# Feed-forwards of a two-layer trunk: the norm's sums pinned in TensorE's order, weight chunks split eight ahead, two plain columns fewer

## The chip, the cores and the metric

The kernel runs on one core of a Trainium2 chip. The metric is the device time of one launch in microseconds (us), the median of several runs; before the change it is 2092.37 us (three runs, 2092.34 to 2093.55). Lower is better.

The engines of the core are TensorE (PE in the profile, its weight loads PEld), VectorE (DVE), ScalarE (ACT), GpSimd (POOL) and SyncE (SP). SP issues the loads of weights; POOL issues the DMAs that add to what lies in memory already ("accumulating" below). Each engine works through its own instructions in the order in which they stand.

## The reference

512 tokens of width 1024 go through two layers. In each layer four parts are added to x, each behind an RMS norm: a feed-forward with weight 1/2, a token mixer, a cross-attention into 256 memory tokens, and a second feed-forward with weight 1/2. What the change touches is the four feed-forwards:

```
def rmsnorm(x, g):
    return x * rsqrt(mean(x * x, -1) + EPS) * g
def swiglu(h, w1, w3, w2):
    return (silu(h @ w1) * (h @ w3)) @ w2
...
x = x + 0.5 * swiglu(rmsnorm(x, ffn1_norm[l]), ffn1_w1[l], ffn1_w3[l], ffn1_w2[l])
```

w1 and w3 are 1024 x 2816 (22 columns j of 128), w2 is 2816 x 1024. Everything is in float32.

## The kernel before, in words

**Layout.** x is kept transposed: eight tiles of 128 channels by 512 tokens (`xall` in the profile). A float32 product is made of three matmuls on rounded halves (`mm3`, L84 to L86): high by high, high by low, low by high. So each weight chunk (128x1024) is split on arrival into `whi` (ScalarE, L76) and `wlo` (DVE, L77), and each operand likewise.

**A norm ahead of its row.** A feed-forward starts before its 1/rms is known. `Norm.part` writes h = gain * x, split into high (ScalarE, L79) and low (DVE, L80), and the first columns are multiplied with this h. In the meantime `Norm.square` sums the squares of the eight channel tiles: the first goes to a tile of its own, `far` (ScalarE, L401), the next three are added to it by accumulating DMAs of POOL (L403), each of which waits for the one before; the fifth starts `sq`, the sixth is added to it and then `far` (DVE, L407 and L409), and the last two are added. The tiles of single squares come from a ring of four buffers. `Norm.tick` is called after every second k of a column product. At its tick `late` it issues the sum over the channels on TensorE (four small matmuls against ones, L346), from which DVE, POOL (power -1/2, `rcol`, L350) and DVE make diagonals `dg` (L357 to L362). `rest` ticks later two matmuls (L369) spread 1/rms over all partitions, ScalarE copies it out (`rrow`, L421), and the epilogues that waited for it (`left`, `right`, L688 to L700) run.

**Two kinds of columns.** The first `PLAIN` columns j of a feed-forward are plain: `col_matmul` makes the product with w1 and the one with w3, 24 matmuls of 128x512 each, and the epilogues multiply by the row. All others are taken two j at a time in the 2x2 Strassen-Winograd form (`Pairs.block`): seven half-size products in place of eight, for w1 and for w3 one block each, of 48 matmuls 128x256 and 12 pairs of matmuls of 512 and 256 columns (L554, L555). The blocks need operands that are made of x times the row (`operands`, DVE and ScalarE, in 14 steps between the plain columns), and sums of weights, one of them by an accumulating DMA of POOL (L134). `PLAIN` is 8, 6, 6, 6 for the four feed-forwards. The columns are made in `PARTS` of 8, 8 and 6; after each part its down-projection (`project`, L451) adds to x, in two halves of four channel tiles. In the last part's projection of a feed-forward the h and the squares of the next norm are made on the way (`late`, `after`): those of the first half's four tiles during the second half.

**Weights.** The list of all chunks is written down in advance (`Weights.src`). `next` hands one out, splits up to `SPLIT` = 5 chunks ahead of it (4 or 6 near blocks) and loads 7 ahead. Raw chunks, split chunks, h, `far`, blocks' operands and others share 38 slots of one pool, so that a load or a split waits until a slot is free.

**What sets the order.** A scheduler puts the instructions of each engine in an order by what is ready when, in its own reckoning, and by the order in which the code issues them. `tc.issue_after(x)` makes instructions of TensorE stand behind instruction x, without a semaphore. Before the change the feed-forwards' sums are not held to a place: two columns can be mixed, and L346 sinks behind them.

Of the kernel before, what the change touches and what calls it, by code (L numbers as in the profile page):

```python
# [14 lines left out]
P = 128  # L15
D = 1024
# [15 lines left out]
PLAIN = (8, 6, 6, 6)  # L32
# [14 lines left out]
def trunk_kernel(ctx: ExitStack, tc: tile.TileContext, ap: dict, out: bass.AP):  # L47
# [33 lines left out]

    def mm3(o, a, b, start, stop, more=False):

        pe.matmul(o, a[0], b[0], start=start, stop=False, skip_group_check=more)  # L84
        pe.matmul(o, a[0], b[1], start=False, stop=False, skip_group_check=more)  # L85
        pe.matmul(o, a[1], b[0], start=False, stop=stop, skip_group_check=more)  # L86


    class Weights:
# [3 lines left out]
        SPLIT, LOAD = 5, 7  # L93

        def __init__(self):
            self.src, self.raw, self.hl, self.at, self.todo = [], {}, {}, 0, []

# [17 lines left out]
        def ahead(self, i, n):  # L115

            m = 0
            while i < len(self.src) and m < n:
                yield i
                m += 2 if len(self.src[i]) == 2 else 1  # L120
                i += 1

# [81 lines left out]
        def next(self):  # L204
            i = self.at
            self.at += 1
            while self.todo:
                self.step()
            block = len(self.src[i]) == 2
            near = any(len(x) == 2 for x in self.src[i:i + 4])  # L210
            end = i >= len(self.src) - 9
            ahead = [*self.ahead(i, (6 if end else 4) if near else self.SPLIT)]
            for j in ahead:
                if j not in self.hl:
                    self.todo.append(self.cut(j))
                    if not block or j == i:
                        while self.todo:
                            self.step()
            for j in self.ahead(i, 5 if end else self.LOAD):
                self.load(j)  # L220
            return self.hl.pop(i)
# [10 lines left out]
    for l in range(L):  # L232
        for w1, w3, w2 in (("ffn1_w1", "ffn1_w3", "ffn1_w2"), ("ffn2_w1", "ffn2_w3", "ffn2_w2")):
            for lo, hi in PARTS:
# [89 lines left out]
    def prepare_mem():  # L324
# [13 lines left out]
        pr = col_to_row(dg, 2)  # L338
# [3 lines left out]
    def col_rsqrt(sq, inv, tag, tile=acc_tile):  # L342

        ps = tile()
        for i in range(NT):
            pe.matmul(ps[:, i:i + 1], sq[:, i * P:(i + 1) * P], ones[:, 0:1], start=True, stop=True)  # L346
# [4 lines left out]
        return col  # L351
# [13 lines left out]
    def col_to_row(dg, n=NT, tile=acc_tile):  # L365

        pr = tile()
        for c in range(2):
            pe.matmul(pr[:, :n * P], ones_r, dg[:, c, :n].rearrange("p a b -> p (a b)"), start=c == 0, stop=c == 1)  # L369
        return pr  # L370

    class Norm:
# [4 lines left out]
        def __init__(self, gain, l, row=True, late=2, rest=2, far=4):  # L377
            self.gain, self.l, self.row, self.late, self.rest, self.FAR = gain, l, row, late, rest, far
# [33 lines left out]
        def tick(self):  # L412
            self.ticks += 1
            if self.ticks == self.late:
                self.col = col_rsqrt(self.sq, 1.0 / D, "rcol")
                if self.row:
                    self.dg = diagonals(self.col)
            if self.ticks == self.late + self.rest and self.row:
                pr = col_to_row(self.dg)
                self.r = tp.tile([P, T], F32, tag="rrow", name="rrow", bufs=1)  # L420
                act.copy(self.r, pr)  # L421
                for fn in self.waiting:
                    fn()

# [38 lines left out]
    def col_matmul(ps, parts, n=T, tick=None):  # L463
        whl = wts.next()
        for k in range(NK):
            mm3(ps[:, :n], (whl[0][:, k, :], whl[1][:, k, :]), parts[k], start=k == 0, stop=k == NK - 1)
            if tick and k % 2:
                tick()
# [731 lines left out]
    norm = Norm("ffn1_norm", 0, late=1, rest=0, far=0)  # L1200
# [30 lines left out]
    for l in range(L):  # L1231
# [11 lines left out]
        norm, nxt = nxt, Norm("ffn2_norm", l)  # L1243
        xattn(l, norm, mn, nxt.add)
        norm = nxt
        if l + 1 < L:
            nxt = Norm("ffn1_norm", l + 1)
# [53 lines left out]
```

## Time and profile before

| | before |
|---|---|
| median of the runs | 2092.37 us |
| the profiled execution's own time | 2092.47 us |
| its span | 2090.7 us |
| TensorE busy | 2077.4 us, 99% |
| weight loads | 1798.0 us, 86% |
| DVE busy | 1408.4 us, 67% |
| ScalarE busy | 918.0 us, 44% |
| POOL busy | 230.3 us, 11% |
| mean granted clock of TensorE | 0.999 |

The span is cut from the first to the last instruction, the time of the run holds 1.8 us around it. A timeline row has the start in us, the duration, engine, line and operation, output<-inputs, sizes and a count; in brackets stands how long the engine was idle before, and what released it. Matmuls overlap: their pace is read from start to start, not from their duration. A row of windows has busy time and number of instructions for PE, PEld, DVE, ACT and POOL in turn, then the granted clock, the share of the DMA engines and GB/s.

### The profile page before, as it was taken

Reading aid. Unit: us, or ns where it says so; the run is one execution under the profiler, and the core shown is the slowest. Engines: PE = TensorE matmul, PEld = TensorE weight load, DVE = VectorE, ACT = ScalarE, POOL = GpSimd, SP = SyncE. Lnnn points to the kernel's source line nnn. Section 1 sums busy time; section 2 is a strip of 40 time slices with the busy share of each in tenths; the row PEclk is TensorE's granted clock in tenths of the full one; section 3 lists DMA queues with packets and bytes.
Section 4 is the critical chain, followed back from the end, with each engine's and each line's share of the span. In section 5 each row is a group of like instructions: output and inputs, shape, how many; then the busy total and the mean of one; then the engine's idle time right before and its main releaser. Section 6 shows DMA issues by size and latency. Waiting matters only on the chain.

```text
span 2090.7 us, 29622 instructions
## 1 busy us (share of the span) xinstructions
PE 2077.4 (99%) x11538; PEld 1798.0 (86%) x11538; DVE 1408.4 (67%) x2126; ACT 918.0 (44%) x1461; POOL 230.3 (11%) x240
## 2 busy tenths in 40 slices
PE   9999999999999999999999999999999999999998
PEld 8889898888888888989888898988788888889897
DVE  7758576687655575766776685758766547668574
ACT  6425345434444343434544353445345434435253
POOL 1100000331000020000020000003410001100000
PEclk9999999999999999999999999999999999999999
DMA  5364554233432246636415646532343331574541
GB/s 188 115 186 121 147 157 156 67 101 108 140 121 87 61 131 186 156 118 176 131 61 158 190 111 184 156 104 71 102 117 130 101 116 41 152 203 129 140 143 71
DMA packets 109533, 268.35 MB, mean 128 GB/s; under 512 B 11536, under 2 KB 14608, under 8 KB 109392
## 3 DMA queue, kind: packets, MB, share of 16 engines
q1 hardware_dynamic: 93952, 224.49, 32.8%
q0 software_dynamic: 13104, 39.07, 10.6%
q10 hardware_dynamic: 2336, 2.89, 0.5%
q8 instruction: 91, 1.49, 0.3%
q14 instruction: 50, 0.41, 0.1%
HBM read 256.70 MB, written 2.10 MB: 124 GB/s over the span
## 4 chain that ended last, share of the span: by engine, by line
PE 97%; DVE 2%; issue 1%; POOL 0%; ACT 0%; POOLq 0%; DVEq 0%; ACTq 0%
PE ps L86 19%; PE ps L84 19%; PE ps L85 18%; PE acc L554 8%; PE acc L84 8%; PE acc L85 8%; PE acc L86 8%; PE acc L555 4%; PE ps L1030 1%; PE ps L1031 1%; PE ps L796 1%; DVE wlo L77 0%; PE ps L979 0%; PE ps L1096 0%; PE acc L346 0%
## 5 line engine op out<-in xcount | busy, mean ns | idle before, releaser
L77 DVE TENSOR_TENSOR wlo<-raw,whi 128x1024 fp32r<-128x1024 f32 (+1 forms) x334 | 394.5, 1202 | 72.0 <-ACT whi L76 63.7
L76 ACT CAST whi<-raw 128x1024 fp32r<-128x1024 f32 (+1 forms) x334 | 330.2, 1017 | 118.1 <-DMA raw<-in_ffn_w_dram 47.6
L85 PE MATMUL ps<-h,whi 128*128 128x512 f32 x848 | 330.0, 389 | 0.0
L84 PE MATMUL ps<-h,whi 128*128 128x512 f32 x848 | 329.9, 391 | 0.0
L86 PE MATMUL ps<-h,wlo 128*128 128x512 f32 x848 | 329.7, 390 | 0.0
L554 PE MATMUL acc<-bhl,whi 128*128 128x512 f32 x744 | 266.3, 398 | 0.0
L86 PE MATMUL ps<-bhl,wlo 128*128 128x256 f32 x744 | 210.8, 284 | 0.2
L85 PE MATMUL ps<-bhl,whi 128*128 128x256 f32 x744 | 209.9, 283 | 0.0
L84 PE MATMUL ps<-bhl,whi 128*128 128x256 f32 x744 | 209.8, 283 | 0.0
L555 PE MATMUL acc<-bhl,wlo 128*128 128x256 f32 x744 | 204.8, 281 | 0.0
L76 ACT CAST whi<-wsum 128x1024 fp32r<-128x1024 f32 x124 | 130.2, 1050 | 151.3 <-DVE wsum L165 83.9
L86 PEld LDWEIGHTS ps<-h,wlo 128*128 128x128 f32 x848 | 159.2, 188 | 33.5
L85 PEld LDWEIGHTS ps<-h,whi 128*128 128x128 f32 x848 | 159.2, 188 | 33.0
L84 PEld LDWEIGHTS ps<-h,whi 128*128 128x128 f32 x848 | 159.1, 188 | 32.9
L77 DVE TENSOR_TENSOR wlo<-wsum,whi 128x1024 fp32r<-128x1024 f32 x124 | 151.5, 1222 | 49.6 <-ACT whi L76 47.3
L554 PEld LDWEIGHTS acc<-bhl,whi 128*128 128x128 f32 x744 | 137.7, 189 | 24.0
L84 PEld LDWEIGHTS ps<-bhl,whi 128*128 128x128 f32 x744 | 141.5, 190 | 4.1
L86 PEld LDWEIGHTS ps<-bhl,wlo 128*128 128x128 f32 x744 | 141.4, 190 | 2.5 <-DVE wlo L77 1.6
L555 PEld LDWEIGHTS acc<-bhl,wlo 128*128 128x128 f32 x744 | 141.0, 190 | 2.8
L85 PEld LDWEIGHTS ps<-bhl,whi 128*128 128x128 f32 x744 | 141.6, 190 | 1.9
L134 POOL DMA_DIRECT2D wsum<-in_ffn_w_dram x62 | 53.8, 867 | 765.0 <-DMA wsum<-in_ffn_w_dram 369.6
L84 PE MATMUL acc<-ahl,whi 128*128 128x512 f32 x328 | 128.0, 390 | 0.0
(272 smaller groups left out, 4127.5 us busy)
## 6 DMA issues: line engine op xcount, KB each, us to landing
raw<-in_ffn_w_dram SPq DMA_DIRECT2D x198, 512.0 KB
wsum<-in_ffn_w_dram SPq DMA_DIRECT2D x124, 256.0 KB
wsum<-in_ffn_w_dram POOLq DMA_DIRECT2D x62, 512.0 KB, 6.7
raw<-in_w_in_dram SPq DMA_DIRECT2D x32, 512.0 KB
raw<-in_ffn_w_dram SPq DMA_DIRECT2D x62, 256.0 KB
raw<-in_w_out_dram SPq DMA_DIRECT2D x16, 512.0 KB
raw<-in_xa_wk_dram SPq DMA_DIRECT2D x16, 512.0 KB
raw<-in_xa_wq_dram SPq DMA_DIRECT2D x16, 512.0 KB
```

Source lines behind the costliest of these rows:

```text
L76: act.copy(hi, src)
L77: dve.tensor_tensor(lo, src, hi.bitcast(F32), op=ALU.subtract)
L84: pe.matmul(o, a[0], b[0], start=start, stop=False, skip_group_check=more)
L85: pe.matmul(o, a[0], b[1], start=False, stop=False, skip_group_check=more)
L86: pe.matmul(o, a[1], b[0], start=False, stop=stop, skip_group_check=more)
L134: nc.gpsimd.dma_start(s1, c2, accum_op=ALU.add)
L554: pe.matmul(ps.rearrange("p (c t) -> p c t", t=HT), w[0], t, start=start and k == 0, stop=False, skip_group_check=True)
L555: pe.matmul(ps[:, :HT], w[1], t[:, 0], start=False, stop=k == 3, skip_group_check=True)
L796: pe.matmul(ps[hh * 64:hh * 64 + 64, o:o + 64], keys[g][:, c:c + 64], b, start=True, stop=True)
L1030: pe.matmul(ps.rearrange("p (c m) -> p c m", m=M), whl[0][:, k], mn[k], start=k == 0, stop=False, skip_group_check=True)
L1031: pe.matmul(ps[:, :M], whl[1][:, k], mn[k][:, 0], start=False, stop=k == NK - 1, skip_group_check=True)
```

## The change

It consists of three parts, all for the four feed-forwards. `PLAIN` goes from (8, 6, 6, 6) to (6, 4, 4, 4): two plain columns j fewer in each, and one pair of blocks more (w1 and w3). `Weights.start` is new: from the last six chunks of the feed-forward before up to the end of the plain columns, up to eight chunks are split ahead and up to ten loaded. And the norms of feed-forwards get `pin`: the sum comes at tick 4 (the end of the first column, instead of tick 2), the row three ticks later, and the first k of each of the next two column products is put behind the pinned matmul, by `issue_after`. The first feed-forward, whose first columns are written out in `begin`, keeps its tick 1 for the sum and gets its row three ticks later.

```diff
-PLAIN = (8, 6, 6, 6)
+PLAIN = (6, 4, 4, 4)
...
+        def start(self, n):
+
+            s = len(self.src)
+            for i in range(s - 6, s + n):
+                self.deep[i] = min(self.DEEP, s + n - i)
...
-            ahead = [*self.ahead(i, (6 if end else 4) if near else self.SPLIT)]
+            ahead = [*self.ahead(i, max((6 if end else 4) if near else self.SPLIT, self.deep.get(i, 0)))]
...
-            for j in self.ahead(i, 5 if end else self.LOAD):
+            for j in self.ahead(i, 5 if end else max(self.LOAD, self.deep.get(i, 0) + 2)):
...
+            if len(wts.src):
+                wts.start(2 * PLAIN[2 * l + (w1 == "ffn2_w1")])
...
         def tick(self):
+
             self.ticks += 1
+            last = None
             if self.ticks == self.late:
-                self.col = col_rsqrt(self.sq, 1.0 / D, "rcol")
+                self.col, last = col_rsqrt(self.sq, 1.0 / D, "rcol")
...
-                pr = col_to_row(self.dg)
+                pr, last = col_to_row(self.dg)
...
+            return last if self.pin else None
...
         whl = wts.next()
+        pin = pinned.pop(0) if pinned else None
         for k in range(NK):
-            mm3(ps[:, :n], (whl[0][:, k, :], whl[1][:, k, :]), parts[k], start=k == 0, stop=k == NK - 1)
-            if tick and k % 2:
-                tick()
+            with tc.issue_after(pin.ins) if pin else nullcontext():
+                mm3(ps[:, :n], (whl[0][:, k, :], whl[1][:, k, :]), parts[k], start=k == 0, stop=k == NK - 1)
+            pin = tick() if tick and k % 2 else None
+            if pin:
+                pinned[:] = [pin] * 2
...
-    norm = Norm("ffn1_norm", 0, late=1, rest=0, far=0)
+    norm = Norm("ffn1_norm", 0, late=1, rest=3, far=0, pin=True)
...
-        norm, nxt = nxt, Norm("ffn2_norm", l)
+        norm, nxt = nxt, Norm("ffn2_norm", l, late=4, rest=3, pin=True)
...
-            nxt = Norm("ffn1_norm", l + 1)
+            nxt = Norm("ffn1_norm", l + 1, late=4, rest=3, pin=True)
```

In all, 384 matmuls of 128x512 go, and 96 of 512 and 480 of 256 columns come.

How the instructions stand, before and after, at the place of which the prediction speaks most: the last down-projection of layer 0 and the start of layer 1's first feed-forward. Lines behind the change are numbered on: L84 to L86 become L86 to L88, L346 L357, L401 L412, L403 L414, L407 and L409 L418 and L420, L451 L465.

TensorE, at the sum of the squares. Before (`ps_9450` is the first column's accumulator, `ps_9526` the second's):

```order
L85 MATMUL ps_9526<-h_9431,whi_9309 128x512
L86 MATMUL ps_9526<-h_9431,wlo_9310 128x512
L346 MATMUL acc_9469<-ones_114,sq_9408 128x1 x4
L84 MATMUL ps_9526<-h_9444,whi_9309 128x512
L85 MATMUL ps_9526<-h_9444,whi_9309 128x512
L86 MATMUL ps_9526<-h_9444,wlo_9310 128x512
```

After (`ps_9674` the first column, `ps_9719` the second):

```order
L86 MATMUL ps_9674<-h_9668,whi_9421 128x512
L87 MATMUL ps_9674<-h_9668,whi_9421 128x512
L88 MATMUL ps_9674<-h_9668,wlo_9422 128x512
L357 MATMUL acc_9703<-ones_114,sq_9632 128x1 x4
L86 MATMUL ps_9719<-h_9557,whi_9427 128x512
L87 MATMUL ps_9719<-h_9557,whi_9427 128x512
```

The sum stood near the end of the second column, which was mixed into the first from its thirteenth matmul on; it now stands behind the first column, which has TensorE to itself, and the second column begins behind it.

ScalarE, during the projection's second half. `sq` and `far` are squares of x tiles, h the high parts of the norm's product, whi of weights. Before, from the whi ahead of the first square to the first square of the projection's second half:

```order
L76 CAST whi<-raw 128x1024 x5
L401 ACTIVATE sq<-xall 128x512 x2
L76 CAST whi<-raw 128x1024
L79 ACTIVATE h<-xall,vec 128x512
L401 ACTIVATE far<-xall 128x512
L79 ACTIVATE h<-xall,vec 128x512
L76 CAST whi<-raw 128x1024
L401 ACTIVATE sq<-xall 128x512
L79 ACTIVATE h<-xall,vec 128x512 x2
L76 CAST whi<-raw 128x1024
L79 ACTIVATE h<-xall,vec 128x512
L401 ACTIVATE sq<-xall 128x512
```

After, from the third square's place on; the square in the fourth row is the first of the second half:

```order
L76 CAST whi<-raw 128x1024
L412 ACTIVATE sq<-xall 128x512
L76 CAST whi<-raw 128x1024 x3
L412 ACTIVATE sq<-xall 128x512
L76 CAST whi<-raw 128x1024
L79 ACTIVATE h<-xall,vec 128x512
L412 ACTIVATE far<-xall 128x512
L79 ACTIVATE h<-xall,vec 128x512
L76 CAST whi<-raw 128x1024
L79 ACTIVATE h<-xall,vec 128x512 x2
L76 CAST whi<-raw 128x1024
L412 ACTIVATE sq<-xall 128x512 x2
```

`far` and the first h stood ahead of every tile of the projection's second half; they now stand behind the first square of that half, and two squares together stand ahead of the last four h.

DVE, at the end of the same projection. xall are the residual adds, h the low parts, sq the adds of squares. Before, from the second half's first residual add to the last square's add:

```order
L451 SCALAR_TENSOR_TENSOR xall<-ps,xall 128x512 x2
L80 SCALAR_TENSOR_TENSOR h<-xall,vec,h 128x512
L451 SCALAR_TENSOR_TENSOR xall<-ps,xall 128x512
L80 SCALAR_TENSOR_TENSOR h<-xall,vec,h 128x512
L407 TENSOR_TENSOR sq<-sq 128x512
L451 SCALAR_TENSOR_TENSOR xall<-ps,xall 128x512
L80 SCALAR_TENSOR_TENSOR h<-xall,vec,h 128x512
L409 TENSOR_TENSOR sq<-sq,far 128x512
L80 SCALAR_TENSOR_TENSOR h<-xall,vec,h 128x512
L407 TENSOR_TENSOR sq<-sq 128x512
L77 TENSOR_TENSOR wlo<-raw,whi 128x1024
L407 TENSOR_TENSOR sq<-sq 128x512
```

After, from the last wlo ahead of the last residual add:

```order
L77 TENSOR_TENSOR wlo<-raw,whi 128x1024
L465 SCALAR_TENSOR_TENSOR xall<-ps,xall 128x512
L80 SCALAR_TENSOR_TENSOR h<-xall,vec,h 128x512 x2
L77 TENSOR_TENSOR wlo<-raw,whi 128x1024
L80 SCALAR_TENSOR_TENSOR h<-xall,vec,h 128x512 x2
L77 TENSOR_TENSOR wlo<-raw,whi 128x1024
L418 TENSOR_TENSOR sq<-sq 128x512
L80 SCALAR_TENSOR_TENSOR h<-xall,vec,h 128x512 x4
L77 TENSOR_TENSOR wlo<-raw,whi 128x1024
L420 TENSOR_TENSOR sq<-sq,far 128x512
L418 TENSOR_TENSOR sq<-sq 128x512 x2
```

Each residual add had its h right behind it; now all the h low parts come behind the last residual add, with wlo between them, and `far` is added later, behind all h.

More of the change, by code (lines that the diff above doesn't have):

```diff
@@ L1 @@
-from contextlib import ExitStack
+from contextlib import ExitStack, nullcontext
 import concourse.bass as bass
@@ L80, in split @@
             dve.scalar_tensor_tensor(lo, src, scale, hi.bitcast(F32), op0=ALU.mult, op1=ALU.subtract)
+    pinned = []
     def mm3(o, a, b, start, stop, more=False):
@@ L89, in trunk_kernel @@
     class Weights:
-        SPLIT, LOAD = 5, 7
+        SPLIT, LOAD, DEEP = 5, 7, 8
         def __init__(self):
             self.src, self.raw, self.hl, self.at, self.todo = [], {}, {}, 0, []
+            self.deep = {}
         def cols(self, w, c):
@@ L337, in prepare_mem @@
         yield
-        pr = col_to_row(dg, 2)
+        pr, _ = col_to_row(dg, 2)
         act.copy(memr, pr[:, :M])
@@ L345, in col_rsqrt @@
         for i in range(NT):
-            pe.matmul(ps[:, i:i + 1], sq[:, i * P:(i + 1) * P], ones[:, 0:1], start=True, stop=True)
+            last = pe.matmul(ps[:, i:i + 1], sq[:, i * P:(i + 1) * P], ones[:, 0:1], start=True, stop=True)
         v = sm.tile([P, NT], F32, tag="v", name="v")
@@ L350, in col_rsqrt @@
         pool.tensor_tensor(col, v, nhalf, op=ALU.pow)
-        return col
+        return col, last
     def diagonals(col, n=NT):
@@ L368, in col_to_row, with __init__ @@
         for c in range(2):
-            pe.matmul(pr[:, :n * P], ones_r, dg[:, c, :n].rearrange("p a b -> p (a b)"), start=c == 0, stop=c == 1)
-        return pr
+            last = pe.matmul(pr[:, :n * P], ones_r, dg[:, c, :n].rearrange("p a b -> p (a b)"), start=c == 0, stop=c == 1)
+        return pr, last
     class Norm:
-        def __init__(self, gain, l, row=True, late=2, rest=2, far=4):
-            self.gain, self.l, self.row, self.late, self.rest, self.FAR = gain, l, row, late, rest, far
+        def __init__(self, gain, l, row=True, late=2, rest=2, far=4, pin=False):
+            self.gain, self.l, self.row, self.late, self.rest, self.FAR, self.pin = gain, l, row, late, rest, far, pin
             self.h = [None] * NK
```

## The prediction

> **What bounds the kernel now.** I read the page first, then TensorE's waits, then the timelines at the places that the change touches.
>
> ```profile
> PE 2077.4 (99%) x11538; PEld 1798.0 (86%) x11538; DVE 1408.4 (67%) x2126; ACT 918.0 (44%) x1461; POOL 230.3 (11%) x240
> PE 97%; DVE 2%; issue 1%; POOL 0%; ACT 0%; POOLq 0%; DVEq 0%; ACTq 0%
> ```
> ```profile
> PE ps L879 <- DVE u L944: 1.1, 2, 0.7
> PE ps L979 <- DVE st L893: 0.8, 2, 0.4
> PE ps L889 <- DVE st L893: 0.4, 2, 0.2
> ```
>
> TensorE is busy 99% of the span, the chain that ended last runs on it for 97%, and between 40 us and the end its listed waits are 2.3 us. So matmul time that goes is gained in full, and each new wait of TensorE is lost in full. All four feed-forwards lie on that one path, and the sum is a count of matmuls plus the new waits. The profiled execution is 2092.47 us (span 2090.7), the median of the three runs 2092.37: the sum is made against 2092.47, and 0.1 us between the two is nothing here. About 0.2%, or 4.2 us, is what a measurement of this kernel can tell from no change: faster is below 2088.2, slower above 2096.6.
>
> **The plain columns.** In each feed-forward two columns j, so four column products of 24 matmuls 128x512, become two blocks of 48 matmuls 128x256 and 12 pairs (512 and 256 wide).
>
> ```profile
> 1042.95 0.39 PE L84 MATMUL ps<-h,whi 128*128 128x512 f32 x1
> ...
> 1048.39 0.39 PE L86 MATMUL ps<-h,wlo 128*128 128x512 f32 x1
> ...
> 1053.15 0.50 PE L346 MATMUL acc<-ones,sq 128*128 128x1 f32 x4
> ```
> ```profile
> 762.71 0.28 PE L84 MATMUL ps<-bhl,whi 128*128 128x256 f32 x1
> ...
> 764.14 0.40 PE L554 MATMUL acc<-bhl,whi 128*128 128x512 f32 x1
> ...
> 766.97 0.28 PE L84 MATMUL ps<-bhl,whi 128*128 128x256 f32 x1
> ```
>
> 1042.95 to 1048.39 is 24 matmuls: 5.44 us, 0.227 each. From 762.71 twelve narrow ones take 1.43 us (0.119 each), then eight pairs 2.83 us (0.354 each). A block is 48 x 0.119 + 12 x 0.354 = 9.97 us. Per feed-forward 4 x 5.44 - 2 x 9.97 = 1.82 us go, four times **7.3 us**. Weight loads stay hidden: these block rows already run load after load.
>
> **The pin, where the output projection of cross-attention stands ahead (second feed-forward of each layer).** Before, the sum of the squares (L346) stands 45 matmuls behind the projection, because the second column is mixed into the first; now 24 behind.
>
> ```profile
> 695.97 0.39 PE L84 MATMUL ps<-h,whi 128*128 128x512 f32 x1
> ...
> 706.18 0.95 PE L346 MATMUL acc<-ones,sq 128*128 128x1 f32 x8
> ```
> ```profile
> 700.95 0.69 DVE L407 TENSOR_TENSOR sq<-sq 128x512 f32<-128x512 f32 x1
> ```
> ```profile
> 708.76 1.29 DVE L362 TENSOR_TENSOR dg<-fixed,chl 128x512 fp32r<-128x512 f32 x2
> ```
>
> TensorE reaches it at 695.97 + 24 x 0.227 = 701.42; the last squares are added at 700.95 + 0.69 = 701.64, some 0.07 to signal: a wait of 0.3 us, in two feed-forwards **0.6 us**. The spreading of 1/rms then comes 18 matmuls (4.1 us and the sum's own 0.8) behind the sum; the diagonals end 3.9 us behind it (706.18 to 710.05): no wait, 1 us to spare. In the first feed-forward nothing of the sum moves; its spreading has about 0.3 us to spare, cost 0 to 0.5, taken as 0.
>
> **The place where it costs: the first feed-forward of layer 1, behind a down-projection.** Split-ahead of 8 takes slots, and the squares, the h parts and `far` get theirs later. ScalarE's queue now holds the first square of the projection's second half ahead of every h and of `far`, DVE's has 12 wlo up to the last square instead of 9, and all eight h lo's stand there behind the last residual add. TensorE has column 1 alone until the pinned sum, nothing to fill in with. Before:
>
> ```profile
> 1029.83 1.03 ACT L76 CAST whi<-raw 128x1024 fp32r<-128x1024 f32 x1
> 1030.77 0.72 ACT L79 ACTIVATE h<-xall,vec 128x512 fp32r<-128x512 f32 x1
> 1031.40 0.61 ACT L401 ACTIVATE far<-xall 128x512 f32<-128x512 f32 x1
> 1031.92 0.71 ACT L79 ACTIVATE h<-xall,vec 128x512 fp32r<-128x512 f32 x1
> ...
> 1039.80 0.72 ACT L79 ACTIVATE h<-xall,vec 128x512 fp32r<-128x512 f32 x1 [3.54 <-DVE xall L451]
> 1040.43 0.62 ACT L401 ACTIVATE sq<-xall 128x512 f32<-128x512 f32 x1
> ```
> ```profile
> 1032.31 0.86 POOL L403 DMA_DIRECT2D far<-sq  x1 [63.75 <-ACT far L401]
> 1037.60 0.86 POOL L403 DMA_DIRECT2D far<-sq  x1 [4.44 <-DMA far<-sq]
> 1041.41 0.85 POOL L403 DMA_DIRECT2D far<-sq  x1 [2.96 <-ACT sq L401]
> ```
> ```profile
> 1039.08 0.69 DVE L451 SCALAR_TENSOR_TENSOR xall<-ps,xall 128x512 f32<-128x512 f32 x1 [1.56 <-PE ps L86]
> ...
> 1041.79 0.69 DVE L451 SCALAR_TENSOR_TENSOR xall<-ps,xall 128x512 f32<-128x512 f32 x1
> 1042.40 0.74 DVE L80 SCALAR_TENSOR_TENSOR h<-xall,vec,h 128x512 fp32r<-128x512 f32 x1
> 1043.06 0.69 DVE L407 TENSOR_TENSOR sq<-sq 128x512 f32<-128x512 f32 x1
> ...
> 1045.16 0.69 DVE L409 TENSOR_TENSOR sq<-sq,far 128x512 f32<-128x512 f32 x1 [0.15 <-DMA far<-sq]
> ...
> 1047.04 1.22 DVE L77 TENSOR_TENSOR wlo<-raw,whi 128x1024 fp32r<-128x1024 f32 x1
> 1048.17 0.68 DVE L407 TENSOR_TENSOR sq<-sq 128x512 f32<-128x512 f32 x1
> ```
>
> These give the steps from start to start: on ScalarE 0.94 for a whi, 0.63 for an h, 0.52 for a square; on DVE 0.61 for a residual add or a square's add, 0.66 for an h lo, 1.13 for a wlo; a `far` DMA to the next 3.81 (5.29 once), the last one to the add that needs it 3.75. In the old clock, up to the projection's end at 1042.95 all is as before. With the new queues:
>
> - ScalarE: square at 1039.80, whi 1040.33, h 1041.27, `far` 1041.90 to 1042.51 (1031.40 before). The DMAs go out at 1042.8, 1046.6, 1050.4. The second square now waits for the first DMA (it takes over that square's buffer), the third for the second, landed at 1046.6 + 3.75 = 1050.4; h of k = 4 is queued behind that one: 1050.9 to 1051.6.
> - DVE: residual adds at 1039.08, 1040.8, 1041.8, 1043.5 with two wlo between, first h lo 1044.1 to 1044.9, second to 1045.5, wlo, third to 1047.3, fourth to 1048.0; lo of k = 4 from 1051.65 to 1052.4, the others 0.66 apart to 1054.4. Then a wlo (its whi 1053.4 to 1054.5), to 1055.7, and three adds: the squares are complete at 1057.6.
> - TensorE: first lo 1.8 us late, third another 1.0, k = 4 waits to 1052.45 where without waits it would stand at 1045.9, and the sum at 1057.65 instead of 1042.95 + 24 x 0.227 = 1048.4. Loss **9.3 us**.
>
> Bounds: with DMAs that never hold anything up, DVE's order alone ends the squares at about 1055.4, 7.0 us; with 5.3 us for each of the first two, 12.3 us. I take 9.3: in the new order fewer loads run beside them, as beside the second one. [...]
>
> **Small things.**
>
> ```profile
> wsum<-in_ffn_w_dram POOLq DMA_DIRECT2D x62, 512.0 KB, 6.7
> ```
>
> POOL now has the accumulating DMA of the first block's weights ahead of 1/rms; it waits only for loads whose slots come free in the middle of the projection, so I take it that POOL is not held; if it is, by up to such a DMA's 6.7 us. SP's loads start earlier at quiet times. The blocks have one place per feed-forward where a wlo is just late:
>
> ```profile
> 889.61 1.23 DVE L77 TENSOR_TENSOR wlo<-wsum,whi 128x1024 fp32r<-128x1024 f32 x1
> ```
>
> ```profile
> 890.57 0.28 PE L85 MATMUL ps<-bhl,whi 128*128 128x256 f32 x1
> 890.89 0.39 PE L86 MATMUL ps<-bhl,wlo 128*128 128x256 f32 x1
> ```
>
> The wlo ends at 890.84, and 0.32 lie between the two matmuls in place of 0.12: 0.2 us lost. In the new order one pair (0.354 us) fewer stands ahead of the second, and the wlo hangs on the same steps: 0 to 0.35 us more in each of four feed-forwards, taken as **1.2** in all, near the upper end.
>
> Sum: -7.3 + 0.6 + 9.3 + 1.2 = +3.8 us, 2092.47 + 3.8 = **2096.3 us**; with its own unknowns (a `far` DMA between 3.6 and 4.4 us, small things 0 to 1.4) 2094.5 to 2097.7.
>
> **The rivals.**
>
> 1. *Slower: the `far` DMAs run beside loads.* At the row of 5.29, both on the path, 3.0 us more: 2099.3. It is told from no change from 0.2 us more per DMA. For: the first DMA took 5.29 with loads beside it. Against: the next took 3.81, and the loads of the deeper split are then done. Chance 0.17.
> 2. *Slower: DVE becomes the bound ahead of the first block.*
>
> ```profile
> 714.60:762.50 47.90, 47.90 (x213) 39.63 (x212) 44.56 (x59) 26.42 (x38) 14.09 (x7) 1.00 0.31 85
> ```
>
> DVE is busy 44.56 of the 47.90 us before the first block; from the row to the first block it now has four columns less, but also the row 21 + 12 matmuls (7.5 us) earlier, so some 33 us for block operands and two blocks' weights. The four columns' own epilogues (4 x 0.6, and two 0.6 splits) go, and eight weight chunks (1.2 each) were split ahead. I find about 2 us to spare. If not: from 1.8 us late a feed-forward has lost what it gained; 2 us in three of them give 2102.3. Chance 0.07.
> 3. *Slower: the clock.* TensorE stands still for 3.4 us at k = 4. Every window of before has a granted clock of 1.00 (as the last row above) and no such gap. At half rate the 11 matmuls behind it would still end ahead of the sum; those behind the sum, 10 or so, would cost 0.23 us more each: 2098.6. [...] Chance 0.06.
> 4. *Same: the chain is shorter*, DVE's order alone counts (7.0): 2094.0. Chance 0.05.
> 5. *Faster: the late order costs nothing*, because the waits at layer 1 are filled. For: 4 us of DVE idling lie in the 20 us before. Against: queues go in order, and column 2 is pinned behind the sum. -7.3 + 0.9 for three starts at 0.3 + 1.2: 2087.3. Chance 0.08.
>
> **How the numbers follow.** My case has 0.57, of which 0.21 lies above 2096.6 and 0.36 below. Rivals 1 to 3 with 0.17, 0.07 and 0.06, of which 0.27 come out slower in the end and 0.03 only as much as no change can hide. Slower: 0.21 + 0.27 = 0.48. Faster: 0.08. Same: 0.36 + 0.03 + 0.05 of rival 4 = 0.44. The range 2092.8 to 2100.3 leaves out rival 5 and the far ends of 1 and 2.
>
> **What would show it.** In the new profile: 384 fewer 128x512 matmuls of h; in the first feed-forward of layer 1 a column that takes about 14.7 us instead of 5.44, with its longest wait for h of ScalarE at k = 4 and a wait of 2.7 us for the squares; `far` written behind the projection's second half; waits of 0.3 us at the sum in the second feed-forwards; the other starts without waits. I am wrong if TensorE waits less than 5 us there (then faster or same), or if more than 2 us of waits stand ahead of first blocks.

## The result, and the profile after

| | before | after |
|---|---|---|
| median | 2092.36 us (14 runs) | 2097.72 us (14 runs, 2095.92 to 2098.87) |
| the profiled execution | 2092.47 us | 2097.61 us |
| its span | 2090.7 us | 2095.8 us |
| mean granted clock of TensorE | 0.999 | 0.997 |

The changed kernel takes 1.0023 times as long (95% interval 1.0016 to 1.003), 5.4 us more. It is slower, clear of noise; the ratio is just beyond the 0.2% that the prediction set as its bound, though the interval reaches a little below it. The time is 1.4 us above the number forecast and inside its range.

The page of the kernel after: busy times, and the chain that ended last by engine.

```profile
PE 2074.9 (99%) x11730; PEld 1801.9 (86%) x11730; DVE 1435.5 (68%) x2202; ACT 939.7 (45%) x1505; POOL 218.8 (10%) x240
PE 94%; DVE 3%; issue 1%; ACT 1%; POOL 0%; DMA 0%; SPq 0%; POOLq 0%; DVEq 0%; ACTq 0%
```

TensorE's waits from 40 us to the end (us in total, times, longest). None of these four stood on the list before.

```profile
PE ps L87 <- DVE h L80: 2.7, 3, 1.6
PE ps L86 <- ACT h L79: 2.2, 1, 2.2
PE ps L88 <- DVE wlo L77: 1.3, 4, 0.3
PE acc L357 <- DVE sq L418: 1.0, 1, 1.0
```

All but the third lie in one column product, the first of layer 1's first feed-forward (k counts its eight channel tiles from 0). TensorE's timeline there, after:

```profile
1039.57 0.39 PE L86 MATMUL ps<-h,whi 128*128 128x512 f32 x1
1041.55 0.50 PE L87 MATMUL ps<-h,whi 128*128 128x512 f32 x1 [1.59 <-DVE h L80]
...
1044.00 0.50 PE L87 MATMUL ps<-h,whi 128*128 128x512 f32 x1 [0.78 <-DVE h L80]
...
1047.67 0.50 PE L86 MATMUL ps<-h,whi 128*128 128x512 f32 x1 [2.24 <-ACT h L79]
...
1053.83 1.05 PE L357 MATMUL acc<-ones,sq 128*128 128x1 f32 x8 [0.99 <-DVE sq L418]
...
1055.80 0.63 PE L87 MATMUL ps<-h,whi 128*128 128x512 f32 x1
1056.23 0.63 PE L88 MATMUL ps<-h,wlo 128*128 128x512 f32 x1
...
1060.56 0.62 PE L380 MATMUL acc<-dg,ones_r 128*128 128x512 f32 x2
```

The 24 matmuls from 1039.57 to 1053.83 take 14.26 us where 5.44 do without waits: 8.8 us lost, with the longest wait at k = 4 for ScalarE's h. From 1055.80 the pace is 0.43 us from start to start instead of 0.227. The windows show why (busy time of PE first, the granted clock third from the end; they are cut where the granted clock changes):

```profile
1045.47:1048.88 3.41, 0.92 (x3) 0.56 (x4) 2.10 (x4) 2.50 (x5) 1.76 (x2) 1.00 0.41 68
1048.88:1052.29 3.41, 3.41 (x10) 2.64 (x9) 3.34 (x6) 2.04 (x3) 0.00 (x0) 0.50 0.98 150
1052.29:1055.71 3.42, 2.43 (x15) 1.86 (x14) 1.54 (x3) 0.00 (x0) 0.54 (x1) 1.00 0.16 30
1055.71:1059.12 3.41, 3.41 (x9) 2.65 (x9) 1.54 (x4) 0.00 (x0) 0.49 (x1) 0.50 0.00 0
```

The clock is granted at half twice, for 3.41 us each time. The first spell ends ahead of the wait for the last square and costs nothing by itself; in the second eight matmuls take 0.2 us more each, 1.6 us. And the accumulating DMAs on POOL's queue, after:

```profile
1039.42 0.86 POOL L414 DMA_DIRECT2D far<-sq  x1 [73.06 <-ACT far L412]
1043.02 0.86 POOL L414 DMA_DIRECT2D far<-sq  x1 [2.73 <-DMA far<-sq]
1046.56 0.86 POOL L414 DMA_DIRECT2D far<-sq  x1 [2.67 <-DMA far<-sq]
```

They go out at the end of the projection's second half, 3.60 and 3.54 us apart, and each lands 3.3 to 3.4 us after its issue. Two small places, the sum in a second feed-forward and a block's late wlo:

```profile
698.95 0.39 PE L88 MATMUL ps<-h,wlo 128*128 128x512 f32 x1
699.45 0.72 PE L357 MATMUL acc<-ones,sq 128*128 128x1 f32 x5
```
```profile
886.88 0.28 PE L87 MATMUL ps<-bhl,whi 128*128 128x256 f32 x1
887.49 0.39 PE L88 MATMUL ps<-bhl,wlo 128*128 128x256 f32 x1 [0.34 <-DVE wlo L77]
```

The first has 0.50 in place of 0.227, 0.27 us lost; the second 0.61 where 0.32 stood before, 0.29 us lost.

### The profile page after: what moved, and what is told of

It is laid out like the page before. It is cut to its first block, busy times and chain, and to the rows that moved or that the text cites. A ratio compares the mean times of both kernels' runs of the same rounds, so it can differ in the third digit from the quotient of the medians.

```text
span 2095.8 us, 30200 instructions
## 1 busy us (share of the span) xinstructions
PE 2074.9 (99%) x11730; PEld 1801.9 (86%) x11730; DVE 1435.5 (68%) x2202; ACT 939.7 (45%) x1505; POOL 218.8 (10%) x240
## 4 chain that ended last, share of the span: by engine, by line
PE 94%; DVE 3%; issue 1%; ACT 1%; POOL 0%; DMA 0%; SPq 0%; POOLq 0%; DVEq 0%; ACTq 0%
PE ps L88 18%; PE ps L86 17%; PE ps L87 17%; PE acc L571 9%; PE acc L86 8%; PE acc L87 8%; PE acc L88 8%; PE acc L572 5%; PE ps L1047 1%; DVE wlo L77 1%; PE ps L1048 1%; PE ps L813 1%; PE ps L996 0%; PE acc L357 0%; PE ps L1113 0%
## 5 line engine op out<-in xcount | busy, mean ns | idle before, releaser
L571 PE MATMUL acc<-bhl,whi 128*128 128x512 f32 x840 | 299.9, 398 | 0.0
L86 PE MATMUL ps<-h,whi 128*128 128x512 f32 x720 | 282.5, 394 | 2.8 <-ACT h L79 2.8
L87 PE MATMUL ps<-h,whi 128*128 128x512 f32 x720 | 281.9, 392 | 2.7 <-DVE h L80 2.7
L88 PE MATMUL ps<-h,wlo 128*128 128x512 f32 x720 | 281.8, 392 | 0.0
L88 PE MATMUL ps<-bhl,wlo 128*128 128x256 f32 x840 | 238.3, 284 | 1.3 <-DVE wlo L77 1.3
L87 PE MATMUL ps<-bhl,whi 128*128 128x256 f32 x840 | 237.0, 283 | 0.0
L86 PE MATMUL ps<-bhl,whi 128*128 128x256 f32 x840 | 236.9, 283 | 0.0
L572 PE MATMUL acc<-bhl,wlo 128*128 128x256 f32 x840 | 233.2, 281 | 0.0
L77 DVE TENSOR_TENSOR wlo<-wsum,whi 128x1024 fp32r<-128x1024 f32 x140 | 170.6, 1219 | 32.8 <-ACT whi L76 32.4
L86 PEld LDWEIGHTS ps<-bhl,whi 128*128 128x128 f32 x840 | 159.7, 190 | 4.6 <-ACT keep L582 0.2
L87 PEld LDWEIGHTS ps<-h,whi 128*128 128x128 f32 x720 | 135.9, 189 | 32.1 <-DVE h L80 3.8
L86 PEld LDWEIGHTS ps<-h,whi 128*128 128x128 f32 x720 | 135.8, 189 | 31.7 <-ACT h L79 3.6
L88 PEld LDWEIGHTS ps<-bhl,wlo 128*128 128x128 f32 x840 | 159.8, 190 | 3.6 <-DVE wlo L77 2.7
L87 PEld LDWEIGHTS ps<-bhl,whi 128*128 128x128 f32 x840 | 159.8, 190 | 1.5
L88 PEld LDWEIGHTS ps<-h,wlo 128*128 128x128 f32 x720 | 136.0, 189 | 28.6
L86 PE MATMUL acc<-ahl,whi 128*128 128x512 f32 x328 | 128.1, 391 | 0.0
```

The source lines that it names most:

```text
L77: dve.tensor_tensor(lo, src, hi.bitcast(F32), op=ALU.subtract)
L571: pe.matmul(ps.rearrange("p (c t) -> p c t", t=HT), w[0], t, start=start and k == 0, stop=False, skip_group_check=True)
L572: pe.matmul(ps[:, :HT], w[1], t[:, 0], start=False, stop=k == 3, skip_group_check=True)
```

## The experiments

One measure serves for all pinned kernels: from the first matmul of layer 1's first h column to the spreading of 1/rms stand 42 matmuls and the sum, 10.48 us when nothing is late. After, it is 1039.57 to 1060.56: 21.0 us. In the kernels without the pin other matmuls stand between, and the measure doesn't hold.

| kernel | pin | two columns fewer | split in advance | accumulating DMAs there | median us | column to spreading |
|---|---|---|---|---|---|---|
| before | no | no | no | yes | 2092.4 | (no pin) |
| after | yes | yes | yes | yes | 2097.7 | 21.0 |
| no_advance | yes | yes | no | yes | 2094.1 | 17.4 |
| advance_not_l1 | yes | yes | not there | yes | 2093.2 | 15.6 |
| advance_no_far | yes | yes | yes | no | 2093.1 | 18.5 |
| filled_waits | yes | yes | yes | yes | 2098.3 | 19.4 |
| no_advance_no_far | yes | yes | no | no | 2087.5 | 10.5 |
| no_advance_six | yes | not there | no | yes | 2096.3 | 17.4 |
| pin_alone | yes | no | no | yes | 2101.8 | 16.8 |
| pin_no_far | yes | no | no | no | 2095.1 | 10.5 |
| plain_alone | no | yes | no | yes | 2116.6 | (no pin) |
| advance_alone | no | no | yes | yes | 2097.0 | (no pin) |
| beside_the_sum | no | no | no | yes, slowed | 2092.5 | (no pin) |

### The split in advance taken away, everywhere and at one place

no_advance:

```diff
-            if len(wts.src):
-                wts.start(2 * PLAIN[2 * l + (w1 == "ffn2_w1")])
```

> The change without its split in advance: the pin and the two plain columns fewer stay, the eight weight chunks go back to the planner's old numbers. Theory A (the split in advance reorders ScalarE and VectorE where layer 1's first feed-forward starts; that column's 8.8 us and a spell of half clock of 1.6 us are its whole price): column 1 of that feed-forward takes less than 8 us instead of 14.3, no half clock there, and the time is 2097.6 - 8.8 - 1.6 = 2087.2 us, about 5 us under the kernel before. Rival B (the pin costs it: the squares' sum and the spreading stand too early): the 14 us column stays, 2096 to 2098 us. Rival C (the column stays cheap, but the first blocks start later without chunks split in advance): the waits move into the first blocks of all four feed-forwards, 2092 us or more.

advance_not_l1:

```diff
-            if len(wts.src):
+            if len(wts.src) and not (l and w1 == "ffn1_w1"):
```

> As the changed kernel, with the split in advance left out at layer 1's first feed-forward alone, the one place that follows a down-projection. Theory A: as without any split in advance, 2087.2 us, within 0.5 us of that kernel, because the other two places pay nothing for it. Rival B (the pin): 2096 to 2098 us. Rival C (the split in advance is what keeps the first blocks fed elsewhere): this kernel is faster than the one without any split in advance by over 1 us.

Measured: 2094.1 us (ratio to before 1.0007, 0.9998 to 1.0015) and 2093.2 us (1.0004, 0.9995 to 1.0013). Theory A fell in its size. The waits that it spoke of are gone, and the two kernels stand within 0.9 us of each other, with overlapping runs (2092.2 to 2094.6 and 2091.9 to 2094.4); but 3.6 and 4.5 us came back, not 10.4. Rival C's number came (2092 or more), but not its place: the first blocks have no new wait. TensorE in the same place of no_advance:

```profile
1044.74 0.39 PE L86 MATMUL ps<-h,whi 128*128 128x512 f32 x1
1046.79 0.50 PE L87 MATMUL ps<-h,whi 128*128 128x512 f32 x1 [1.65 <-DVE h L80]
1047.12 0.40 PE L88 MATMUL ps<-h,wlo 128*128 128x512 f32 x1
1049.13 1.87 PE L355 MATMUL acc<-ones,sq 128*128 128x1 f32 x8 [1.61 <-DVE sq L416]
...
1055.27 0.60 PE L87 MATMUL ps<-h,whi 128*128 128x512 f32 x1
```

Now the column's last h is late (k = 7), then the last square, and the granted clock is 0.50 from 1048.89 to 1055.72, so that the matmuls behind the sum come 0.43 us apart. POOL's queue of the same kernel:

```profile
1029.34 0.86 POOL L412 DMA_DIRECT2D far<-sq  x1 [63.61 <-ACT far L410]
1035.83 0.86 POOL L412 DMA_DIRECT2D far<-sq  x1 [5.64 <-DMA far<-sq]
1040.09 0.85 POOL L412 DMA_DIRECT2D far<-sq  x1 [3.40 <-ACT sq L410]
```

The accumulating DMAs go out early again, but they land late. The times of the three from issue to landing, in the kernel before and then here (shortest, median, longest):

```profile
DMA to landing us min/median/max: 3.3/3.7/5.0
DMA to landing us min/median/max: 3.7/5.2/6.2
```

In order they are 5.0, 3.3 and 3.7 us before, and 6.2, 3.7 and 5.2 here. (From the second issue to the third it is more, 3.81 and 4.26, because the third waits for its square from ScalarE too.) VectorE's add of `far`, with the last h lo queued behind it, starts at 1045.38, 5.3 us after the third issue. A second chain had stood behind the one that I undid.

### The accumulating DMAs taken away, the split in advance kept

```diff
-            nxt = Norm("ffn1_norm", l + 1, late=4, rest=3, pin=True)
+            nxt = Norm("ffn1_norm", l + 1, late=4, rest=3, far=0, pin=True)
```

> As the changed kernel, but layer 1's first feed-forward has none of its squares added by the accumulating DMAs (far=0): VectorE adds all of them, ScalarE copies none for GpSimd. It tells which engine's order makes the column late. Theory A in its detail (ScalarE's copies and its eight h stand behind the first square of the projection's second half, and the chain of DMAs of 3.6 us each holds the later squares): the 2.24 us wait at k=4 goes, the waits for VectorE's low parts at k=2 and for the last square stay, some 5 us in all, the clock stays up: about 2092.4 us. Rival D (VectorE with its three more low parts of weights is what is late): the time stays at 2097 us or goes up, since VectorE gets more adds.

Measured: 2093.1 us (1.0006, 0.9997 to 1.0015), near the 2092.4 expected; the profiled execution is one of the longer ones, 2095.3. The wait at k = 4 went, as expected. The wait for the last square, which was to stay, went too: the sum stands 13 matmuls behind the column's start in this kernel, not 24, and waits for nothing. What is left are two waits for h lo (k = 0 and k = 2), and a clock that did not stay up.

```profile
1043.24 0.50 PE L87 MATMUL ps<-h,whi 128*128 128x512 f32 x1 [2.36 <-DVE h L80]
1046.31 0.80 PE L87 MATMUL ps<-h,whi 128*128 128x512 f32 x1 [0.65 <-DVE h L80]
```
```profile
1047.29:1050.71 3.42, 3.42 (x14) 2.96 (x12) 3.42 (x6) 1.20 (x2) 0.00 (x0) 0.50 0.00 0
```

This half clock lasts 10.24 us, and it is not in every execution: the four with a mean granted clock of 0.996 take 2095.3 to 2096.5 us, the seven with 0.997 to 0.999 take 2091.8 to 2093.3. The median is of the second kind, the profile of the first.

So VectorE's own order, which rival D named, is part of the lateness with the split in advance, and the DMAs another.

### TensorE kept busy in the waits

```diff
+FILL = {2: 3, 4: 9}
...
+            if fill and k in fill:
+                t = acc_tile()
+                for _ in range(fill[k]):
+                    with tc.issue_after(prev.ins):
+                        prev = pe.matmul(t[:, :P], ones, ones, start=True, stop=True)
+                pin = prev
```

> As the changed kernel, with twelve 128x128 matmuls of ones that nobody reads, put into the waits of layer 1's first column (three at k=2, nine at k=4). The data come no earlier; only TensorE's records fill up. Theory A with the clock as a consequence of the waits: the two spells of half clock (granted 0.51 and 0.52) go; the first lies ahead of a wait for the last square and hides there, the second gives back its 8 matmuls x 0.2 us = 1.6 us: 2096.0 us. Rival E (the clock falls for another reason, or these small matmuls do not count as work): granted clock 0.5 in the same windows, 2097.6 us. Rival F (it was fewer matmuls in flight, not waiting, that held the h back): over 4 us less.

The granted clock of filled_waits at the same place, in three windows of 3.41 us:

```profile
1047.07:1050.48 3.41, 2.91 (x17) 2.20 (x17) 2.13 (x5) 3.28 (x6) 1.76 (x2) 1.00 0.52 80
1050.48:1053.89 3.41, 1.61 (x7) 0.94 (x6) 3.26 (x5) 1.27 (x2) 0.00 (x0) 1.00 0.88 150
1053.89:1057.31 3.42, 2.65 (x16) 2.35 (x17) 1.06 (x4) 0.00 (x0) 1.03 (x1) 1.00 0.00 0
```

No half clock is left at this place in this execution, but that the filling did it is not shown. The wait for the last square is not filled and even grew to 2.57 us, and the clock stays at 1.00 behind it. Of the 2.91 us in the first window some 1.2 are filling. And three of the other six executions have a mean granted clock of 0.997, as the kernel after with its two spells, instead of 0.998. From the column to its sum it takes 14.25 us as it did after (14.26), since the data come no earlier; from the column to the spreading 19.4 instead of 21.0, the 1.6 us expected. The whole time does not show it: 2098.3 us (2097.1 to 2100.2, 7 runs) against 2097.7. In the profile TensorE waits 1.5 us for u in the token mixers where it waits 0.4 after, which eats most of the gain. Why the other executions with 0.998 are no faster stays open.

### The accumulating DMAs taken away without the split in advance; six plain columns kept

no_advance_no_far is no_advance with `far=0` in the same line as above:

> As the kernel without the split in advance, and at layer 1's first feed-forward VectorE adds all squares, with no accumulating DMA. Theory G (found in the kernel without the split in advance: the three accumulating DMAs took 6.5, 4.3 and 5.3 us there instead of 5.3, 3.8 and 3.7 before, because the loads of the first block's weights, asked for two columns earlier, move beside them; the last h and the last square come late, 6.9 us with the half clock behind them): the waits at that column's end go and the time is 2094.1 - 6.9 = 2087.2 us. Rival H (it is VectorE that is late there, and it now gets three adds of 0.69 us more): 2093 us or more. Rival I (the pinned sum itself is too early, whoever adds the squares): a wait of over 1 us in front of the sum stays, 2090 us or more.

no_advance_six is no_advance with

```diff
-PLAIN = (6, 4, 4, 4)
+PLAIN = (6, 4, 6, 4)
```

> As the kernel without the split in advance, but layer 1's first feed-forward keeps its six plain columns, the other three have two fewer. Theory G: the loads of its first block stay where they were before, so the accumulating DMAs take 3.7 to 3.8 us again and the last h is in time; the sum, pinned behind the eighth group, waits 0.5 us or so for the last square (which ended at 1048.85 us before, while the column ended at 1048.4 us). 2094.1 - 6.9 + 1.8 (the columns kept) + 0.5 = 2089.5 us. Rival I (the pin alone makes the waits): they stay, 2094.1 + 1.8 = 2095.9 us.

no_advance_no_far takes **2087.5 us** (0.9975, 0.9965 to 0.9985): 5.2 us less than the kernel before and 10.2 less than after. The sum and the spreading in its timeline:

```profile
1045.69 0.94 PE L355 MATMUL acc<-ones,sq 128*128 128x1 f32 x8
1050.73 0.62 PE L378 MATMUL acc<-dg,ones_r 128*128 128x512 f32 x2
```

No wait, 5.44 us behind the column's start at 1040.25. That is theory G's number to 0.3 us, and rivals H and I are out. no_advance_six, however, takes 2096.3 us (1.0017, 1.0008 to 1.0026), rival I's number, with the same two waits of 1.6 us. Theory G as I had put it, that the loads move because the blocks start two columns earlier, was wrong: here the blocks start where they did, and the loads go out beside the DMAs all the same (which land after 6.9, 3.5 and 4.6 us).

### The pin alone, with and without the accumulating DMAs

pin_alone is the kernel before with the change's code for the pin only (`PLAIN = (8, 6, 6, 6)`, no `wts.start`); pin_no_far has `far=0` in addition.

> The kernel before with the pin alone: old plain columns, no split in advance. Theory G: three waits of 0.3 to 0.5 us for the last square and nothing else, as the loads do not move: 2092.4 + 0.9 to 1.5 = 2093.3 to 2093.9 us. Rival I (the pin costs it by itself): a late h and 2 us or more at layer 1's first feed-forward, 2096 us or more.

> The kernel before with the pin alone, and VectorE adds all squares at layer 1's first feed-forward (far=0). Theory G (in the kernel with the pin alone the weight loads go out at 1038.4 and 1043.8 us instead of 1042.5 and 1051.3, right beside the accumulating DMAs, which then take 5.6, 5.6 and 4.9 us; the 6.3 us lost there come of that alone): both waits go, 2101.8 - 6.3 = 2095.5 us or a little less. Rival I (the pinned sum is too early, whoever adds the squares): over 1 us of wait in front of the sum stays, 2098 us or more.

Measured: 2101.8 us (1.0041, 1.0028 to 1.0053), rival I's number, and 2095.1 us (1.0011, 1.0002 to 1.0021), theory G's, with no wait at that start. The pin alone makes the late h and the late sum, but only while the accumulating DMAs are there. The 2.5 us that pin_no_far still takes more than the kernel before lie elsewhere: 1.1 us of it are listed waits for split weights at the blocks' pairs (L569 and L570); the rest was not followed. POOL's queue in pin_alone, then two weight loads on SP's queue there, then SP's load of the kernel before at that point:

```profile
1032.96 0.86 POOL L412 DMA_DIRECT2D far<-sq  x1 [63.28 <-ACT far L410]
1038.59 0.86 POOL L412 DMA_DIRECT2D far<-sq  x1 [4.78 <-DMA far<-sq]
1044.23 0.85 POOL L412 DMA_DIRECT2D far<-sq  x1 [4.79 <-ACT h L79]
```
```profile
1038.36 0.33 SPq L149 DMA_DIRECT2D raw<-in_ffn_w_dram  x1
...
1043.80 0.33 SPq L149 DMA_DIRECT2D raw<-in_ffn_w_dram  x1
```
```profile
1042.47 0.33 SPq L140 DMA_DIRECT2D raw<-in_ffn_w_dram  x1
```

With the pin a load of 512 KB goes out 0.2 and 0.4 us ahead of the second and the third DMA; they land after 5.1 and 4.8 us (VectorE's add starts at 1049.12). Before, no load starts near the second, which lands after 3.3 us, and the load of 1042.47 starts 1.1 us after the third, which lands after 3.7. That the pin moves loads at all comes through the slots: in the program of before the load of 1042.47 waits for one of the projection's last matmuls to leave its slot, and with the pin the load in its place waits for a matmul 4 us earlier. That it is the new order of the program that deals the slots this way is argued, not tried.

The other half of the pin's price is in TensorE's order. Here are the places, in the order of the program, of the column's start, of the first use of its last h (h_9444) and of the squares' sum, in the kernel before and in pin_alone:

```
5427 L84 MATMUL ps_9450<-h_9339,whi_9271 128x512
...
5457 L84 MATMUL ps_9450<-h_9444,whi_9271 128x512
...
5472 L346 MATMUL acc_9469<-ones_114,sq_9408 128x1 x4
```
```
5425 L86 MATMUL ps_9450<-h_9339,whi_9271 128x512
...
5446 L86 MATMUL ps_9450<-h_9444,whi_9271 128x512
...
5449 L355 MATMUL acc_9481<-ones_114,sq_9408 128x1 x4
```

Before, parts of column 2 are mixed in: the last h is wanted 30 matmuls (6.8 us) behind the start, the sum 45 (10.2 us). Pinned, it is 21 (4.8 us) and 24 (5.4 us). The low half of that h, which is the one that comes late, is wanted 34 matmuls (7.7 us) behind the start before, and 22 (5.0 us) pinned. The slack that is gone, 2.7 us for it and 4.8 for the sum, had covered the accumulating DMAs.

### Transfers put beside the accumulating DMAs, no pin

```diff
             if 0 < self.n < self.FAR:
+                if self.l == 1 and self.gain == "ffn1_norm":
+                    for c in range(2):
+                        nc.sync.dma_start(out[0, c * P:(c + 1) * P, :512], s)
                 nc.gpsimd.dma_start(self.far, s, accum_op=ALU.add)
```

> The kernel before, with two 256 KB copies of the same squares to the output array (the final rows overwrite them later) put on SyncE's queue beside each of the three accumulating DMAs of layer 1's first feed-forward; nothing else is edited. Theory G (another transfer started with it slows the accumulating DMA): each takes 5 to 7 us instead of 5.3, 3.8 and 3.7, the last h comes 3 us late and TensorE waits for it with no pin at all: 2095 to 2098 us. Rival K (the DMAs are slow for another reason, such as when in the projection they are issued): 3.7 to 3.9 us for the second and third, and 2092 to 2093.5 us.

POOL's queue, VectorE's add of `far` and the h lo behind it, and the window of the first two DMAs:

```profile
1032.08 0.86 POOL L406 DMA_DIRECT2D far<-sq  x1 [63.20 <-ACT far L401]
1038.44 0.86 POOL L406 DMA_DIRECT2D far<-sq  x1 [5.51 <-DMA far<-sq]
1045.49 0.85 POOL L406 DMA_DIRECT2D far<-sq  x1 [6.19 <-issue]
```
```profile
1048.86 0.69 DVE L412 TENSOR_TENSOR sq<-sq,far 128x512 f32<-128x512 f32 x1 [4.07 <-DMA far<-sq]
1049.46 0.75 DVE L80 SCALAR_TENSOR_TENSOR h<-xall,vec,h 128x512 fp32r<-128x512 f32 x1
```
```profile
1031.55:1045.00 13.45, 13.45 (x62) 11.12 (x60) 10.72 (x15) 7.71 (x12) 1.71 (x2) 1.00 0.99 320
```

The DMA engines are busy 0.99 of the window, where the same window of the kernel before has 0.54, and the first two accumulating DMAs land after 6.1 and 6.5 us, before after 5.0 and 3.3; the third, behind the crowd, after 3.3. That half of theory G is shown. The other half falls: the time is 2092.5 us (1.0, 0.9991 to 1.0009), with no wait. The last h lo is ready at 1050.2; unpinned, TensorE wants it 34 matmuls behind 1042.73, at 1050.4. Slow DMAs alone cost nothing here, with 0.2 us to spare, and neither does an early sum alone (pin_no_far has no wait there); together they cost the 6.3 us by which pin_alone exceeds 10.48. Part of the 6.3 is the clock: it is granted at 0.50 from 1051.19 to 1058.02 there, and TensorE works in 5.15 us of that, behind the wait for the sum, so some 2.6 us by estimate.

### The plain columns alone, the split in advance alone

plain_alone is the kernel before with

```diff
-PLAIN = (8, 6, 6, 6)
+PLAIN = (6, 4, 4, 4)
```

> The kernel before with two plain columns fewer in each feed-forward and nothing else. Theory (the pin is what lets the blocks start two columns earlier: unpinned, the sum and the spreading stand late in TensorE's order, the row of 1/rms comes when the first block's h already ask for it): waits over 1 us in the first blocks of the feed-forwards, 10 us in all against the 7.1 us that the columns give: 2095 to 2104 us, no better than the kernel before. Rival (the row is in time without the pin): 2085 to 2090 us.

advance_alone is the kernel before with `start`, `deep` and the call of `wts.start` alone.

> The kernel before with the split in advance alone. Theory A: it costs at layer 1's first feed-forward whatever stands beside it, as it did with the pin (2097.7 against 2094.1 us, and 2093.1 against 2087.5 us without the accumulating DMAs): 4 to 6 us more than the kernel before, 2096 to 2098.5 us. Rival J (it costs only together with the pin, which makes TensorE wait for the last square in its eighth group): within 1 us of the kernel before.

plain_alone: 2116.6 us (1.0115, 1.01 to 1.0131), far worse than expected, and not quite by the mechanism named. TensorE's waits in it:

```profile
PE ps L86 <- DVE wlo L77: 14.9, 16, 4.2
PE ps L84 <- ACT whi L76: 5.6, 4, 1.4
```

Without the pin the blocks that start two columns earlier find their weights not split. That the late row of 1/rms holds up VectorE's and ScalarE's queues ahead of those splits is likely, but no run here tries it. The profile fits: in layer 0's second feed-forward VectorE idles 5.4 us until the row is there at 722.6, then has no gap until 756.0, and the wlo for which TensorE waits until 739.47 stands in that stretch, between the blocks' operands. advance_alone: 2097.0 us (1.0018, 1.0009 to 1.0027), the number of theory A, but not at its place. In its timeline two of the waits:

```profile
1068.90 0.50 PE L86 MATMUL ps<-h,whi 128*128 128x512 f32 x1 [1.40 <-DVE t L705]
1120.91 0.50 PE L571 MATMUL acc<-bhl,whi 128*128 128x512 f32 x1 [1.07 <-ACT whi L76]
```

The start of the column loses only some 1.2 us; the rest falls behind the late row of 1/rms and in the first blocks. The split in advance costs with the pin and without it, by different waits.

## Why the prediction came out as it did

- **The plain columns.** Forecast -7.3. 384 matmuls of h went (848 to 720 at each of the three lines of `mm3`). At the paces of the new trace, 0.227 and 0.120 with 0.354 a pair, it is -7.1. Right.
- **The pin in the second feed-forwards.** Forecast +0.6; 0.27 twice, 0.5. The 0.07 us that the forecast counts from the last add to the sum were 0.05 (699.40 to 699.45). Right.
- **Layer 1's first feed-forward.** Forecast a column of 14.7 us and a loss of 9.3; it took 14.26 and lost 8.8. With the whole place 3.38 us earlier than in the old clock, the DMAs were due at 1039.4, 1043.2 and 1047.0, and went out at 1039.42, 1043.02 and 1046.56; the sum was due at 1054.3 and stood at 1053.83. The chain by single instructions held: the longest wait at k = 4, for ScalarE. Two pieces of it came out shorter. At k = 4 the loss was 3.0 us, not 3.7, since the second DMA freed its square's buffer 3.4 us after its issue and not 3.75. And the wait for the last square was 1.0 instead of 2.7 us; 1.4 of the difference went into the half clock ahead of it.
- **What a DMA takes.** The 3.81 of the forecast is a step from issue to issue, and about half a microsecond of it was a wait for ScalarE's square: that DMA landed after 3.3 us. For the steps of 3.60 and 3.54 that came in its place the forecast's size was near enough.
- **The clock.** Rival 3 had a chance of 0.06, a stretch of 3.4 us in which TensorE stands still as its condition, and 0.23 us for some ten matmuls behind the sum as its price; that such a stretch would bring half rate I had assumed; no row that I gave shows it. It came as an addition to my case, 0.2 for eight, 1.6 us. This is the term that the sum lacked. It came without such a stretch: the longest gap was 2.24 us, TensorE was busy 0.92 and 2.43 us of the 3.41 ahead of the two spells, and in no_advance two gaps of 1.65 and 1.61 us stand beside 6.83 us of half clock. I had also written that every window of before has a granted clock of 1.00; in the trace of before it is 0.50 from 2084.91 on, near its end, 4.0 us behind the end of the last matmul (2080.90).
- **The blocks' late wlo.** Forecast +1.2; 0.29 four times, 1.2. Right.
- **The sum.** -7.1 + 0.5 + 8.8 + 1.6 + 1.2 = +5.0, against +5.1 between the two profiled executions. That it closes to 0.1 us is in part luck: the wait for u in the token mixers is 0.7 us shorter after (0.4 instead of 1.1), and the sum does not have it.
- **Rival 1**, slow accumulating DMAs, did not happen in this kernel: steps of 3.60 and 3.54 us, for the reason given (the loads were done). It is the second-latest chain, though, and it becomes the latest as soon as the split in advance is gone.
- **Where the prediction was wrong without its number showing it**: it laid the whole loss on the split in advance, and priced the pin at 0.6 us. The pin alone costs 9.1 us (2101.8 - 2092.7; 8.0 between the profiled executions), 6.3 of them at this one start. I had noted that before the sum stood 45 matmuls behind the start because column 2 was mixed in, and used it for the second feed-forwards alone. My first experiment, which should have given back 10.4 us, showed it.
- **Rival 5** named the price of a version without this loss, 2087.3. no_advance_no_far, which takes both chains away, has 2087.5, by other means: rival 5 had the waits filled.

## What to carry to other kernels

A pin is priced by the first use of every operand that the free order had put later, not only by the instruction that is pinned: here it took 2.7 us of slack from the last h lo and 4.8 from the sum, and a helper on another queue that had been free stood on the path. Where two chains are late at one place, undoing one shows the other: the split in advance was worth 3.6 us with the accumulating DMAs and 5.6 without, the DMAs 4.6 and 6.6, both together 10.2 (the kernels with waits have half clock in these times, and not the same in every execution: the mean granted clock of advance_no_far lies between 0.996 and 0.999). And parts of a change can need each other: two columns fewer cost 24 us without the pin; with it the pair brought 5, once the split in advance and the accumulating DMAs at one place were out of the way.

## What the runs showed of the hardware that was not expected

- An accumulating DMA of 256 KB landed 3.3 us after its issue when no weight load on SP's queue started near it (the second one before, all three after to 0.1 us), and after 4.8 to 6.2 us when a weight load had gone out up to 0.6 us ahead of it (5.0 the first one before, 6.2 and 5.2 the first and the third of no_advance, 5.1 and 4.8 the second and the third of pin_alone). With the DMA engines at 0.99, in beside_the_sum, two landed after 6.1 and 6.5.
- TensorE's clock was granted at half where its waits were well under the 3.4 us of rival 3: in the kernel after for 3.41 us twice, with no gap longer than 2.24 us, in no_advance for 6.83 us, with gaps of 1.65 and 1.61, and in advance_no_far for 10.24 us, with gaps of 2.36 and 0.65. Ahead of half clock TensorE was busy 0.92 us of 3.41 (after, up to 1048.88) and 1.04 us of 3.40 (advance_no_far, up to 1043.85), but also 2.43 us of 3.42, of which 1.05 the sum (after, up to 1055.71). In filled_waits 3.41 us with 1.61 us of work, up to 1053.89, are followed by full clock. What decides it is not shown.
- The clock was not the same in every execution of one kernel: four of the eleven of advance_no_far have a mean of 0.996 and take 2095.3 to 2096.5 us, seven 0.997 to 0.999 and 2091.8 to 2093.3 us. A microsecond or two between two kernels with such waits may come of this and not of the edit.
